# FFN up product by Strassen's scheme, and the residual kept in DRAM, in a one-core hybrid layer

## The chip, the core and the metric

One NeuronCore of a Trainium2 chip runs the whole program. The time is device microseconds of one execution; lower is better. The kernel before was timed three times on the chip, and one more execution was taken by the hardware profiler.

## The reference

One layer on a latent stream of 1024 tokens by 1024 features, with 256 context tokens ahead of it. A token mixer comes first (state-space heads, Fourier mixing, pooling, one output projection), then a feed-forward part that the change is about:

```
a = h @ w_up                      # 1024x1024 @ 1024x5632
a = depthwise 3x3 convolution of a, on a grid of 16 rows x 64 columns, plus bias
val, gate = split(a)              # 2 x 2816 channels
y = (gelu(gate) * val) @ w_down   # 1024x2816 @ 2816x1024
out = layer_norm(ALPHA * x + g2 * y) * ln2_g + ln2_b
```

All inputs and the output are float32.

## The kernel before, in words

Every large product is done in three matmuls: each float32 operand is split into a high part (rounded by ScalarE to fp32r) and a low part (the rest, by GpSimd or VectorE), and high*high, high*low and low*high are added in PSUM. `split` does this. One matmul has a 128x128 stationary part and 512 moving columns.

The feed-forward part works on 22 pairs of channel tiles (`NPAIR`), each a value tile and the gate tile that belongs to it, 44 tiles of 128 channels in all. For a tile, `up_weights` loads 512 KB of `w_up` and splits it, and L1233 does 8 (k tiles) x 3 x 2 (halves q of the tokens, 512 each) = 48 matmuls into a PSUM tile `pu` of 128x1024. There are three PSUM tiles of that size, and two of 128x512. `h2h` and `h2l` are the two parts of the transposed activations.

`conv2d` reads `pu`: ScalarE writes the centre tap with the bias to `cv` (L1176), and VectorE adds the other eight taps, one instruction each (L1184). After the gate tile, ScalarE does the gelu (L1251), GpSimd multiplies by the value (L1252), and the product is split into `gh` and `gl`. `w_down` rows of the pair are loaded, multiplied by the gate vector `g2b` on GpSimd (L1256) and split.

Two pairs make a group. Its down product is cut into 16 units (8 token tiles t, 2 column halves nb): `down_unit` does 6 matmuls into a 128x512 PSUM tile `pdn` (L1158), and VectorE adds it to the residual `xa[t]`, which stays in SBUF (L1161, L1163 the first time). A unit is taken after every second k of an up tile (from tile 6, k 3, to tile 39), so that up and down matmuls alternate; 9 units are left for after the last up tile. There are 9 groups and 144 units; the last four pairs (18 to 21) are multiplied at the end by `last_mm` (L1282, 192 matmuls, `pl`), four token tiles with the pairs taken in turn, then four more, each followed by its layer norm (`post_early`, `post_late`).

The order of instructions on each engine is laid out when the program is built: a planner takes them in program order, but passes over those whose inputs are not due yet by its own costs; `tc.issue_after` adds an edge on one engine. On the chip, each engine and the DMA queue of SP then run their list in that fixed order.

Of the kernel before, what the change touches and what calls it, by code (L numbers as in the profile page):

```python
# [33 lines left out]
def hybrid_layer(  # L34
# [179 lines left out]
    def split(raw, hi, lo, eng=None):  # L214

        S.activation(hi, raw, AF.Identity)  # L216
        (eng or G).tensor_tensor(lo, raw, hi.bitcast(F32), op=ALU.subtract)  # L217
# [856 lines left out]
    def post1(t):
# [3 lines left out]
        V.scalar_tensor_tensor(xa[t], xa[t], st[1], lnb, op0=ALU.mult, op1=ALU.add)  # L1078
# [44 lines left out]
    def up_weights(n):
        ct = chan[n]
        raw = ring("ht2", f"wur{ct}", [P, KD, P])
        nc.sync.dma_start(raw, w_up[:, ct * P : (ct + 1) * P].rearrange("(k p) n -> p k n", p=P))
# [20 lines left out]

    def down_unit(u):

        group, t, nb = u  # L1150
# [4 lines left out]
        for _, gh, gl, wh, wl in group:
            a, b = gh[:, t * P : (t + 1) * P], gl[:, t * P : (t + 1) * P]
            for u_, v_ in ((a, wh), (a, wl), (b, wh)):
                TE.matmul(pt, u_, v_[:, s], start=i == 0, stop=i == n - 1)  # L1158
                i += 1
        if (t, nb) in seen:  # L1160
            V.tensor_tensor(xa[t][:, s], xa[t][:, s], pt, op=ALU.add)  # L1161
# [253 lines left out]
```

## Time and profile before

| | |
|---|---|
| median of 3 runs | 1222.45 us (1218.78 to 1223.37) |
| profiled execution | 1218.48 us, of which the span from first to last instruction is 1216.7 us |
| mean granted TensorE clock | 0.987 |
| TensorE busy | 1154.5 us, 95% |
| VectorE, ScalarE, GpSimd busy | 942.2, 384.3, 455.8 us |
| first up matmul of the feed-forward part (L1194) | at 461.51 us |
| last up matmuls (L1233) | at 1147.21 us |

PE is TensorE, PEld its weight loads, DVE VectorE, ACT ScalarE, POOL GpSimd, SP the engine that issues the DMAs. A row of a timeline has the start, the time, the engine, the line, the operation, output<-inputs, the count, and in brackets how long the engine had been idle and what released it. A row of a table of stages has the length, and for each engine its busy time and instructions.

### The profile page before, as it was taken

To read this page: it belongs to the slowest core of one execution; us is meant where nothing else is said; L and a number is where in the kernel's file an instruction comes from. 1 tells how busy PE (TensorE), PEld (TensorE's weight loads), DVE (VectorE), ACT (ScalarE), POOL (GpSimd) and SP (SyncE) were. 2 spreads that over 40 slices of the span, in tenths; PEclk is the share of its full clock that TensorE was granted. 3 is DMA by queue.
4 is the path that set the end of the run, shared out by engine and by line. 5 is a ranking of instruction groups with operands and counts; after the bars stand their busy time and mean duration, and the time that the engine had idled before them with its cause. 6 is when DMAs were issued, how large, how long until landed. Compare 5 with 4: busy or idle time off the path is not lost.

```text
span 1216.7 us, 14285 instructions
## 1 busy us (share of the span) xinstructions
PE 1154.5 (95%) x5463; PEld 939.9 (77%) x5463; DVE 942.2 (77%) x1360; ACT 384.3 (32%) x575; POOL 455.8 (37%) x243
## 2 busy tenths in 40 slices
PE   4999999899878998999999999999999999999996
PEld 2798887777756787788888888888888888888884
DVE  5788787698898889898777776767777777777947
ACT  2263576711433133332221222221212222222144
POOL 0010122354262044565353535343443535353146
PEclk9999999899988999999999999999999999999998
DMA  9848575566624111221111212021121102121013
GB/s 320 295 141 313 158 211 154 176 216 193 221 78 165 42 36 52 87 70 52 35 52 35 69 35 60 27 69 35 41 64 35 55 33 70 35 69 35 18 36 138
DMA packets 104779, 122.51 MB, mean 101 GB/s; under 512 B 7021, under 2 KB 83579, under 8 KB 104711
## 3 DMA queue, kind: packets, MB, share of 16 engines
q1 hardware_dynamic: 104711, 121.60, 31.3%
q8 instruction: 43, 0.70, 0.2%
q14 instruction: 25, 0.20, 0.1%
HBM read 106.82 MB, written 14.76 MB: 100 GB/s over the span
## 4 chain that ended last, share of the span: by engine, by line
PE 76%; DVE 14%; DMA 5%; ACT 2%; issue 2%; POOL 1%; SPq 0%; DVEq 0%; POOLq 0%; ACTq 0%
PE pu L1233 37%; PE pdn L1158 16%; PE pout L1008 4%; PE pz L342 4%; PE px L443 3%; PE pl L1282 3%; DMA bc<-cs_scratch 2%; PE pf L443 1%; PE pu L1194 1%; DMA wa<-in_w_ada_dram 1%; DVE xa L1077 1%; DVE y L918 1%; PE pm L296 1%; DMA zb_r<-in_w_in_dram 1%; DVE h2h L203 1%
## 5 line engine op out<-in xcount | busy, mean ns | idle before, releaser
L1184 DVE SCALAR_TENSOR_TENSOR cv<-pu,ffc,cv 128x945 f32<-128x945 f32 (+7 forms) x368 | 432.6, 1177 | 21.1 <-ACT cv L1176 11.4
L1233 PE MATMUL pu<-h2h,wul 128*128 128x512 f32 x656 | 205.4, 394 | 0.0
L1233 PE MATMUL pu<-h2h,wuh 128*128 128x512 f32 x656 | 205.1, 394 | 0.0
L1233 PE MATMUL pu<-h2l,wuh 128*128 128x512 f32 x656 | 204.4, 393 | 0.0
L1161 DVE TENSOR_TENSOR xa<-xa,pdn 128x512 f32<-128x512 f32 x128 | 87.4, 683 | 128.2 <-PE pdn L1158 127.9
L217 POOL TENSOR_TENSOR wul<-wur,wuh 128x1024 fp32r<-128x1024 f32 x44 | 106.8, 2429 | 204.3 <-ACT wuh L216 204.2
L1233 PEld LDWEIGHTS pu<-h2h,wuh 128*128 128x128 f32 x656 | 123.2, 188 | 29.0
L1233 PEld LDWEIGHTS pu<-h2l,wuh 128*128 128x128 f32 x656 | 123.2, 188 | 28.6
L1233 PEld LDWEIGHTS pu<-h2h,wul 128*128 128x128 f32 x656 | 123.2, 188 | 27.9
L216 ACT ACTIVATE wuh<-wur 128x1024 fp32r<-128x1024 f32 x44 | 46.3, 1054 | 240.0 <-PE pu L1233 220.7
L1158 PE MATMUL pdn<-wdh,gl 128*128 128x512 f32 x288 | 113.3, 393 | 0.0
L1158 PE MATMUL pdn<-wdl,gh 128*128 128x512 f32 x288 | 113.2, 393 | 0.0
L1158 PE MATMUL pdn<-wdh,gh 128*128 128x512 f32 x288 | 113.1, 393 | 0.0
L1256 POOL TENSOR_TENSOR wdr<-wdr,g2b 128x1024 f32<-128x1024 f32 x22 | 53.1, 2412 | 68.2 <-DMA wdr<-in_ffn_w_down_dram 68.2
L1252 POOL TENSOR_TENSOR cv<-cv,cv 128x1024 f32<-128x1024 f32 (+1 forms) x23 | 53.1, 2310 | 60.6 <-ACT cv L1251 60.6
L217 POOL TENSOR_TENSOR gl<-cv,gh 128x1024 fp32r<-128x1024 f32 (+1 forms) x23 | 53.4, 2322 | 42.3 <-ACT gh L216 41.1
L1158 PEld LDWEIGHTS pdn<-wdh,gh 128*128 128x128 f32 x288 | 54.1, 188 | 12.9
L1158 PEld LDWEIGHTS pdn<-wdh,gl 128*128 128x128 f32 x288 | 54.1, 188 | 12.4
L1158 PEld LDWEIGHTS pdn<-wdl,gh 128*128 128x128 f32 x288 | 54.1, 188 | 12.3
L1176 ACT ACTIVATE cv<-pu,ffc 128x1024 f32<-128x1024 f32 (+3 forms) x46 | 53.2, 1156 | 29.0 <-PE pu L1233 18.8
L1251 ACT ACTIVATE cv<-cv 128x1024 f32<-128x1024 f32 (+1 forms) x23 | 23.5, 1021 | 119.4 <-DVE cv L1184 119.4
L217 POOL TENSOR_TENSOR wdl<-wdr,wdh 128x1024 fp32r<-128x1024 f32 x22 | 52.8, 2413 | 4.7 <-ACT wdh L216 4.7
(357 smaller groups left out, 2082.2 us busy)
## 6 DMA issues: line engine op xcount, KB each, us to landing
wur<-in_ffn_w_up_dram SPq DMA_DIRECT2D x44, 512.0 KB
wad<-in_w_ada_dram SPq DMA_DIRECT2D x32, 512.0 KB
wdr<-in_ffn_w_down_dram SPq DMA_DIRECT2D x22, 512.0 KB
wa<-in_w_ada_dram SPq DMA_DIRECT2D x32, 256.0 KB
bc<-cs_scratch SPq DMA_DIRECT2D x32, 256.0 KB
xr<-in_x_dram SPq DMA_DIRECT2D x8, 512.0 KB
wx_r<-in_w_in_dram SPq DMA_DIRECT2D x8, 512.0 KB
m_scratch<-EU SPq DMA_DIRECT2D x16, 256.0 KB
```

The costliest lines, as they stand in the source:

```text
L216: S.activation(hi, raw, AF.Identity)
L217: (eng or G).tensor_tensor(lo, raw, hi.bitcast(F32), op=ALU.subtract)
L342: TE.matmul(pt[:, j * 512 : j * 512 + ZW], a, b[:, k % 4, :], start=first and i == 0, stop=last and i == 2)
L443: TE.matmul(pt[:, q * 512 : q * 512 + 512], a[:, k, :], b[q][:, k, :], start=k == 0 and i == 0, stop=k == KD - 1 and i == 2)
L1008: TE.matmul(pt[:, nb * 512 : nb * 512 + 512], u, v[:, nb * 512 : nb * 512 + 512], start=first and i == 0, stop=last and i == 2)
L1158: TE.matmul(pt, u_, v_[:, s], start=i == 0, stop=i == n - 1)
L1161: V.tensor_tensor(xa[t][:, s], xa[t][:, s], pt, op=ALU.add)
L1176: S.activation(acc[:, a * 64 : b * 64], pt[:, a * 64 : b * 64], AF.Identity, bias=ffc[:, 396 + ct : 397 + ct], scale=ffc[:, 176 + ct : 177 ...
L1184: last = V.scalar_tensor_tensor(dst, pv[:, r0 + dy : r1 + dy, c0 + dx : c1 + dx], ffc[:, w * 44 + ct : w * 44 + ct + 1], dst, op0=ALU.mult ...
L1233: TE.matmul(pt[:, q * 512 : q * 512 + 512], a[:, k, :], b[q][:, k, :], start=k == 0 and j == 0, stop=k == KD - 1 and j == 2)
L1252: G.tensor_tensor(acc[:, s], acc[:, s], acc_v[:, s], op=ALU.mult)
L1256: G.tensor_tensor(raw, raw, g2b, op=ALU.mult)
```

## The change

For pairs 0 to 6 (`PS` = 7) the up product stays as it was. From pair 7 on (the eighth) a pair is one product with two channel tiles as rows and the two token halves as columns. Of its 8 k tiles, two (0 and 1) are multiplied as before; the other six make two blocks of three, and this 2x2 by 2x2 block product is done with seven block products instead of eight, in Winograd's form of Strassen's scheme. A block product has 3 x 3 = 9 matmuls, so a pair has 63 + 24 = 87 matmuls instead of 96.

- Sums of activations (`combine`, 8 sums and 3 splits for each of three k, on VectorE with ScalarE, in pairs 3 to 5, and `last_t4` after pair 6) go to nine tiles T.
- Sums of weights (`pair_sums`, four sums and five splits on GpSimd with ScalarE for each pair) go to three buffers `S1`, `S2`, `S3`, written for the next pair after the last use in this one; `pair_gate` splits five k tiles of the gate weights.
- `pair` lays out the products. ScalarE copies a partial sum from one PSUM bank to another three times for each pair (X to Z, Z to Y, Z to W), and the product `p7` to SBUF, from where VectorE adds it to both halves of the gate tile. `p7` uses one of the two small PSUM tiles that the units use.
- Eight units are taken in each pair from pair 3 to 20 (`slot`), which is all 144, so none is left for after the last up tile.
- The residual is in DRAM (`xd`): each unit loads its 256 KB, adds, and stores them; the loads are issued three units ahead, into five buffers. It is loaded to SBUF again before `last_mm`.
- `w_down` is loaded and split in halves; three sets of gate buffers instead of four.
- In the last pair the two vertical taps of the convolutions are products on ScalarE that GpSimd adds, and VectorE does six taps instead of eight.

The core of the diff:

```diff
+        nc.sync.dma_start(xd[t * P : (t + 1) * P, :], xa[t])
...
+    KS, PS, TS = 3, 7, 3
+    KD0 = KD - 2 * KS
+    K2, K1 = KD0, KD - KS
...
+    loaded = {}
+    def down_load(u):
+        group, t, nb = u
+        key = group[0][0], t, nb
+        if key not in loaded:
+            loaded[key] = post.tile([P, 512], F32, tag="xt", name=f"xt{group[0][0]}_{t}_{nb}", bufs=5)
+            nc.sync.dma_start(loaded[key], xd[t * P : (t + 1) * P, nb * 512 : nb * 512 + 512])
+        return loaded[key]
...
         group, t, nb = u
+        xt = down_load(u)
+        for v in units[:3]:
+            down_load(v)
+        xs = xd[t * P : (t + 1) * P, nb * 512 : nb * 512 + 512]
         pt = psb(f"pdn{group[0][0]}_{t}_{nb}")
         n = 3 * len(group)
         i = 0
-        s = slice(nb * 512, nb * 512 + 512)
-        for _, gh, gl, wh, wl in group:
+        for _, gh, gl, wd in group:
             a, b = gh[:, t * P : (t + 1) * P], gl[:, t * P : (t + 1) * P]
-            for u_, v_ in ((a, wh), (a, wl), (b, wh)):
-                TE.matmul(pt, u_, v_[:, s], start=i == 0, stop=i == n - 1)
+            for u_, v_ in ((a, 0), (a, 1), (b, 0)):
+                TE.matmul(pt, u_, wd[nb][:, v_, :], start=i == 0, stop=i == n - 1)
                 i += 1
         if (t, nb) in seen:
-            V.tensor_tensor(xa[t][:, s], xa[t][:, s], pt, op=ALU.add)
+            V.tensor_tensor(xt, xt, pt, op=ALU.add)
         else:
-            V.scalar_tensor_tensor(xa[t][:, s], xa[t][:, s], ALPHA, pt, op0=ALU.mult, op1=ALU.add)
+            V.scalar_tensor_tensor(xt, xt, ALPHA, pt, op0=ALU.mult, op1=ALU.add)
             seen.add((t, nb))
-    lastv = [None]
-    def conv2d(pt, ct, rows, acc=None):
+        nc.sync.dma_start(xs, xt)
...
+        own = taps
+        if off:
+            own = [d for d in taps if d[1]]
+            up, dn = off
+            S.activation(up[:, 64:T], pt[:, 0 : T - 64], AF.Identity, scale=factor(-1, 0))
+            vtap[0] = S.activation(dn[:, 0 : T - 64], pt[:, 64:T], AF.Identity, scale=factor(1, 0))
+        def add(a, b):
+            for r0, r1, t in ((max(a, 1), b, up), (a, min(b, 15), dn)):
+                s = slice(r0 * 64, r1 * 64)
+                G.tensor_tensor(acc[:, s], acc[:, s], t[:, s], op=ALU.add)
...
+    def combine(k):
+        ta, b22 = qt("q5", f"ta{k}", [P, 2, 512]), tb[:, 0, :]
+        def whole(dst, q, kt):
+            eng().tensor_tensor(dst, h2h[q][:, kt, :].bitcast(F32), h2l[q][:, kt, :].bitcast(F32), op=ALU.add)
+        b11, b12, b21 = ta[:, 0, :], ta[:, 1, :], t4raw(k)
+        whole(b11, 0, K1 + k)
+        whole(b12, 1, K1 + k)
+        whole(b22, 1, K2 + k)
+        whole(b21, 0, K2 + k)
+        eng().tensor_tensor(b11, b12, b11, op=ALU.subtract)
+        eng().tensor_tensor(b12, b22, b12, op=ALU.subtract)
+        eng().tensor_tensor(b22, b22, b11, op=ALU.subtract)
+        eng().tensor_tensor(b21, b21, b22, op=ALU.subtract)
+        for j, src in ((0, b11), (1, b22), (2, b12)):
+            split(src, Tt[j][k][:, 0, :], Tt[j][k][:, 1, :], eng())
+    def last_t4():
+        for k in range(KS):
+            split(t4raw(k), h2h[1][:, K1 + k, :], h2l[1][:, K1 + k, :], eng())
...
+    STAG = ("q5", "q7", "q13")
...
+    def pair_sums(i):
+        v, g = raws[i]
+        s1, s2, s3 = [qt(tag, f"S{j}_{i}", [P, 8, P], F32R) for j, tag in enumerate(STAG)]
+        sw[i] = {j: [(t[:, k, :], t[:, 3 + k, :]) for k in range(KS)] for j, t in ((1, s1), (2, s2), (3, s3))}
+        sw[i][4] = [(s1[:, 6, :], s3[:, 6, :]), (s1[:, 7, :], s3[:, 7, :]), (s2[:, 6, :], s2[:, 7, :])]
+        a11, a12, a21, a22 = v[:, K1 : K1 + KS, :], v[:, K2 : K2 + KS, :], g[:, K1 : K1 + KS, :], g[:, K2 : K2 + KS, :]
+        G.tensor_tensor(a21, a21, a22, op=ALU.add)
+        G.tensor_tensor(a11, a21, a11, op=ALU.subtract)
+        split(a11, s2[:, 0:3, :], s2[:, 3:6, :])
+        split(a21, s1[:, 0:3, :], s1[:, 3:6, :])
+        G.tensor_tensor(a12, a12, a11, op=ALU.subtract)
+        split(a12[:, 0:2, :], s1[:, 6:8, :], s3[:, 6:8, :])
+        split(a12[:, 2:3, :], s2[:, 6:7, :], s2[:, 7:8, :])
+        G.tensor_tensor(a11, a22, a11, op=ALU.subtract)
+        split(a11, s3[:, 0:3, :], s3[:, 3:6, :])
+    def pair_gate(i):
+        n = KD - KS
+        wh, wl = qt("X0", f"gwh{i}", [P, n, P], F32R), qt("EM1", f"gwl{i}", [P, n, P], F32R)
+        g = raws[i][1]
+        split(g[:, 0:n, :], wh[:], wl[:])
+        gw[i] = wh, wl
...
+    def first_product(i):
+        pv[i] = psa(f"pu{chan[2 * i]}")
+        X, Z = pv[i][:, 0:512], pv[i][:, 512:1024]
+        mm(X, wk(vw[i], K1), hk(0, K1), True)
+        zc[i] = S.copy(Z, X)
+    def pair(i, mid):
+        more = i + 1 < NPAIR
+        if i not in pv:
+            first_product(i)
+        X, Z = pv[i][:, 0:512], pv[i][:, 512:1024]
+        mm(X, wk(vw[i], K2), hk(0, K2))
+        mm(X, wk(vw[i], 0, KD0), hk(0, 0, KD0))
+        if more:
+            slot()
+        mm(Z, sk(i, 2), tk(2))
+        pq[i] = psa(f"pu{chan[2 * i + 1]}")
+        Y, W_ = pq[i][:, 0:512], pq[i][:, 512:1024]
+        S.copy(Y, Z)
+        if more:
+            slot()
+        p7 = psb(f"p7_{i}")
+        mm(p7, sk(i, 3), tk(3), True)
+        s7 = post.tile([P, 512], F32, tag="s7", name=f"s7_{i}")
+        s7c = S.copy(s7, p7)
+        if more:
+            with tc.issue_after(s7c.ins):
+                pair_value(i + 1)
+            slot()
+        mm(Z, sk(i, 1), tk(1))
+        seed = seedw[0] = S.copy(W_, Z)
+        with tc.issue_after(seed.ins):
+            mid()
+            down_split()
+        slot()
+        def z_end():
+            mm(Z, sk(i, 4), hk(1, K2))
+            mm(Z, wk(vw[i], 0, KD0), hk(1, 0, KD0))
+        if more:
+            mm(Y, wk(gw[i], K2), hk(1, K1))
+            slot()
+            z_end()
+            slot()
         else:
+            z_end()
+        acc_v = conv2d(pv[i], chan[2 * i], [(0, 16)], off=None if more else (ring("ht2", "cu0"), ring("ht2", "cd0")))
+        if more:
+            with tc.issue_after(tap[0].ins):
+                pair_sums(i + 1)
+            if i + 2 < NPAIR:
+                pair_raw(i + 2, 0)
+            first_product(i + 1)
+            slot()
         else:
+            mm(Y, wk(gw[i], K2), hk(1, K1))
+        mm(Y, wk(gw[i], 0, KD0), hk(0, 0, KD0))
+        if more:
+            slot()
+        mm(W_, wk(gw[i], 0, KD0), hk(1, 0, KD0))
+        if more:
+            with tc.issue_after(zc[i + 1].ins):
+                pair_gate(i + 1)
+            if i + 2 < NPAIR:
+                pair_raw(i + 2, 1)
+        pqv = pq[i][:].rearrange("p (a n) -> p a n", a=2)
+        V.tensor_tensor(pqv, pqv, s7.unsqueeze(1).broadcast_to([P, 2, 512]), op=ALU.add)
+        return acc_v
+    gtags = [("X1", "X2"), ("X3", "q6"), ("q10", "q11")]
...
+    def down_raw(i, nb, tag=0):
+        s = slice(nb * 512, nb * 512 + 512)
+        raw = post.tile([P, 512], F32, tag="wdr", name=f"wdr{i}_{nb}", bufs=2)
+        nc.sync.dma_start(raw, w_down[i * P : (i + 1) * P, s])
+        G.tensor_tensor(raw, raw, g2b[:, s], op=ALU.mult)
+        half_done.append((i, nb, tag, raw))
...
+        j = i - 1
+        if j < 0:
+            return
+        gated(j, *accs_.pop(j))
+        if j < LASTG:
+            if j % 2 == 1:
+                grp = [(m, *gates[m], wds[m]) for m in (j - 1, j)]
+                units.extend((grp, t, nb) for nb in range(2) for t in range(NT))
+                for m in (j - 1, j):
+                    down_raw(m, 1)
+            else:
+                for m in (j, j + 1):
+                    down_raw(m, 0)
+        else:
+            for m in {LASTG: (0,), LASTG + 1: (1,)}.get(j, ()):
+                down_raw(LASTG, m)
+                down_raw(LASTG + 1, m)
...
+                if n == 2 * PS - 1:
+                    pair_raw(PS, 0)
+                    pair_raw(PS, 1)
+                    pair_value(PS)
...
+            down_split()
+            between(i)
+            if TS <= i < TS + KS:
+                with tc.issue_after(lastv[0].ins):
+                    combine(i - TS)
+            if i == PS - 1:
+                last_t4()
+                pair_sums(PS)
+                pair_raw(PS + 1, 0)
+                pair_gate(PS)
+                pair_raw(PS + 1, 1)
+        else:
+            acc_v = pair(i, lambda: between(i))
+            if i < NPAIR - 1:
+                acc = conv2d(pq[i], chan[2 * i + 1], [(0, 16)])
+            else:
+                acc = conv2d(pq[i], chan[2 * i + 1], [(0, 8), (8, 16)], off=(qt("q3", "cu1"), qt("wl0", "cd1")), early=True)
...
+    for t, tag in enumerate(STAG + ("q2", "X0", "EM1", "q4", "wh0")):
+        xa[t] = qt(tag, f"xl{t}")
+        nc.sync.dma_start(xa[t], xd[t * P : (t + 1) * P, :])
+    down_split()
+    LT = iter(("q9", "q12", "q14", "q8"))
+    for m in range(LASTG + 2, NPAIR):
+        with tc.issue_after((vtap if m == NPAIR - 1 else seedw)[0].ins):
+            for nb in range(2):
+                down_weights(m, nb, next(LT), V if m == NPAIR - 1 else None)
+    gated(NPAIR - 1, *accs_.pop(NPAIR - 1), tags=("q0", "q1"))
...
-        last_acc(t, t != 2)
+        last_acc(t, t != 1)
```

More of the change, by code (lines that the diff above doesn't have):

```diff
@@ new lines, in hybrid_layer, with t4raw @@
+    Tt = [[qt(next(TTAG), f"T{j}_{k}", [P, 2, 512], F32R) for k in range(KS)] for j in (1, 2, 3)]
+    t4r, tb = qt("q13", "t4r", [P, 2, 512]), qt("q7", "tb", [P, 2, 512])
+    eng = cycle(V)
+    def t4raw(k):
+        return t4r[:, k, :] if k < 2 else tb[:, 1, :]
+    def combine(k):
[13 more added lines that the diff above has]
+            split(src, Tt[j][k][:, 0, :], Tt[j][k][:, 1, :], eng())
@@ new lines, in pair_gate, with mm @@
+    def pair_gate(i):
[4 more added lines that the diff above has]
+        gw[i] = wh, wl
+    def mm(dst, a, b, start=False):
+        n = len(a)
+        for k in range(n):
+            for j, (u, w) in enumerate(((0, 0), (0, 1), (1, 0))):
+                TE.matmul(dst, a[k][u], b[k][w], start=start and k == 0 and j == 0, stop=k == n - 1 and j == 2,
+                          skip_group_check=True)
@@ new lines, in wk, with sk, hk, tk @@
+    def wk(w, k0, n=KS):
+        return [(w[0][:, k, :], w[1][:, k, :]) for k in range(k0, k0 + n)]
+    def sk(i, j):
+        return sw[i][j]
+    def hk(q, k0, n=KS):
+        return [(h2h[q][:, k, :], h2l[q][:, k, :]) for k in range(k0, k0 + n)]
+    def tk(j):
+        return [(t[:, 0, :], t[:, 1, :]) for t in Tt[j - 1]]
+    pv, pq, zc = {}, {}, {}
+    def first_product(i):
[3 more added lines that the diff above has]
+        zc[i] = S.copy(Z, X)
@@ L1258, in hybrid_layer, with between @@
-        split(raw[:], wdh[:], wdl[:])
-        group.append((i, gh, gl, wdh, wdl))
-        if len(group) == 2 and i < NPAIR - 3:
-            queue = [(list(group), t, nb) for t in range(NT) for nb in range(2)]
-            group = []
+        gates[i] = gh, gl
+    LASTG = NPAIR - 4
+    accs_ = {}
+    def between(i):
+        j = i - 1
[15 more added lines that the diff above has]
+                down_raw(LASTG + 1, m)
@@ L1268, in hybrid_layer @@
         down_unit(u)
+    for t, tag in enumerate(STAG + ("q2", "X0", "EM1", "q4", "wh0")):
[8 more added lines that the diff above has]
+    gated(NPAIR - 1, *accs_.pop(NPAIR - 1), tags=("q0", "q1"))
+    group = [(m, *gates[m], wds[m]) for m in range(LASTG, NPAIR)]
     NG = len(group)
@@ L1304, in post_sum @@
         for p_, s in parts_of(t):
[L1305 removed]
+            with tc.issue_after(lastv[0].ins) if t == 0 else ExitStack():
+                V.tensor_tensor(xa[t][:, s], xa[t][:, s], p_, op=ALU.add)
     def post_early(t):
```

141 lines of the change are left out of this document (88 added, 53 removed).

## The prediction

> **What bounds the kernel now.** I read the page's engine table, the clock row and the chain first, then a table of stages, the groups of the feed-forward part, and timelines of its two ends. The profiled execution took 1218.48 us, 1.78 us more than its span and 4 us below the median of the runs (1222.45); the sum is made against it. Under 0.5% (6 us) a run of this kernel can't be told from no change.
>
> ```profile
> span 1216.7 us, 14285 instructions
> PE 1154.5 (95%) x5463; PEld 939.9 (77%) x5463; DVE 942.2 (77%) x1360; ACT 384.3 (32%) x575; POOL 455.8 (37%) x243
> ...
> PE 76%; DVE 14%; DMA 5%; ACT 2%; issue 2%; POOL 1%; SPq 0%; DVEq 0%; POOLq 0%; ACTq 0%
> ```
> ```profile
> 527.00:538.00 11.00, 11.00 (x49) 8.94 (x48) 10.72 (x10) 5.01 (x5) 8.37 (x4) 1.00 0.33 95
> 566.00:583.00 17.00, 17.00 (x75) 13.83 (x75) 14.95 (x16) 3.10 (x3) 4.81 (x2) 1.00 0.10 32
> 583.00:599.00 16.00, 16.00 (x71) 13.03 (x70) 12.02 (x12) 3.22 (x4) 7.21 (x3) 1.00 0.11 33
> 600.00:700.00 100.00, 100.00 (x434) 81.13 (x433) 72.71 (x73) 23.21 (x22) 45.48 (x19) 1.00 0.18 53
> 1147.00:1160.00 13.00, 13.00 (x58) 10.63 (x57) 11.88 (x18) 1.86 (x3) 0.00 (x0) 1.00 0.00 0
> 1160.00:1172.00 12.00, 12.00 (x54) 9.64 (x53) 6.00 (x9) 3.26 (x5) 9.56 (x5) 1.00 0.14 46
> 1190.00:1200.00 10.00, 10.00 (x44) 8.07 (x43) 6.69 (x22) 7.96 (x14) 9.39 (x5) 1.00 0.15 58
> 1200.00:1208.00 8.00, 4.82 (x21) 3.57 (x19) 8.00 (x28) 1.65 (x3) 7.84 (x4) 1.00 0.48 192
> ```
> ```profile
> 603.59 2.77 PE pu L1233 x12
> 610.51 1.39 PE pdn L1158 x6
> ```
>
> The chain is TensorE for 76%. In the stage rows (length, then busy time of PE, PEld, DVE, ACT, POOL) PE is busy all of 600 to 700 us, with 434 matmuls in 100 us, and stays so until about 1205. The chain's pieces give the price: 12 up matmuls 2.77 us, 6 down matmuls 1.39 us, 0.231 us each either way. A pair costs 96 + 48 = 144 matmuls, 33.2 us. VectorE has 73% of the time filled, ScalarE 23%, GpSimd 45%. So in pairs 7 to 21 a matmul taken away is worth 0.231 us as long as nothing else sets the pace.
>
> **The products.** 15 pairs with 87 matmuls for 96: 135 fewer, 135 x 0.231 = **31.2 us off**. The other matmuls keep number, shape and weight loads. A pair with its 8 units is then 135 matmuls, 31.2 us.
>
> **What each pair gains in other work.**
>
> ```profile
> L1184 DVE SCALAR_TENSOR_TENSOR cv<-pu,ffc,cv 128x945 f32<-128x945 f32 x120 | 144.1, 1201 | 6.1 <-ACT cv L1176 2.1
> L1161 DVE TENSOR_TENSOR xa<-xa,pdn 128x512 f32<-128x512 f32 x118 | 80.5, 683 | 124.4 <-PE pdn L1158 124.4
> L1184 DVE SCALAR_TENSOR_TENSOR cv<-pu,ffc,cv 128x1008 f32<-128x1008 f32 x60 | 75.9, 1264 | 1.1
> L1184 DVE SCALAR_TENSOR_TENSOR cv<-pu,ffc,cv 128x960 f32<-128x960 f32 x60 | 72.9, 1215 | 1.1
> L217 POOL TENSOR_TENSOR wul<-wur,wuh 128x1024 fp32r<-128x1024 f32 x30 | 72.3, 2410 | 170.9 <-ACT wuh L216 170.9
> L1176 ACT ACTIVATE cv<-pu,ffc 128x1024 f32<-128x1024 f32 x30 | 35.7, 1191 | 0.0
> ```
> ```profile
> 1178.44 1.22 DVE L1305 TENSOR_TENSOR xa<-xa,pl 128x1024 f32<-128x1024 f32 x1 [12.23 <-PE pl L1282]
> 1187.47 0.57 ACT L1294 COPY pl<-xa 128x512 f32<-128x512 f32 x1
> ```
>
> *VectorE.* 16 taps (8 x 1.201 + 4 x 1.215 + 4 x 1.264 = 19.5 us), 8 unit adds (5.5) and the new add of `p7`, 1.22 by the L1305 row: 26.2 us in a pair of 31.2, 84% where it was 75% (25.0 of 33.2). It stays below PE. Counted from a pair's start, the value tile is complete after 96 matmuls (22.2 us); its taps and the adds among them end near 35.5, 4.3 us into the next pair, where ScalarE wants that PSUM tile for Y after 30 matmuls (6.9 us); PE needs Y's copy only 21 matmuls later. The gate's taps end near 19 us of the next pair, and PE wants the tile after 102 (23.6 us). Some 3 to 4 us of slack at both places: cost 0. If that cover goes, VectorE sets the pace: each us that it loses beyond it costs one us a pair.
>
> *ScalarE.* Four copies of 128x512 (0.57 each by the L1294 row) and some nine smaller splits bring it to about 12 us a pair. Each copy lies between two products: Y must be read before Z is written again 21 matmuls later (4.9 us), Z for the next pair 24 matmuls ahead (5.5 us). An instruction ahead in its queue takes 1.2 us at most. Cost 0, except in the last pair, where no units lie between, and W is needed at once: about 1 us.
>
> *GpSimd.* By 2.41 us for 1024 columns: value split 2.4, four sums of 384 (3.6), sum splits 1536 columns (3.6), gate split 640 (1.5), the down weights and gating as before (9.6): 20.7 us, 66%. The sums may start only when the value tile ends (22.2 us) and S2, S3 are wanted 60 and 75 matmuls later (13.9 and 17.3 us); up to there they cost 2.9 and 7.7 us of GpSimd. Hidden. With three gate buffers, each odd pair's `gh` waits for the last unit of an older group; from there to the new group's sixth matmul lie 26 matmuls, 6.0 us, against ScalarE 1.06 + GpSimd 2.41. Up to 1 us in each of seven groups; I take 1 us in all.
>
> *The residual through DRAM.*
>
> ```profile
> 805.32 0.34 SPq L1255 DMA_DIRECT2D wdr<-in_ffn_w_down_dram  x1
> 809.66 2.42 POOL L1256 TENSOR_TENSOR wdr<-wdr,g2b 128x1024 f32<-128x1024 f32 x1 [4.37 <-DMA wdr<-in_ffn_w_down_dram]
> ```
>
> A 512 KB load is used 4.3 us after its issue, at 53 GB/s. Each unit now moves 512 KB in two transfers, about every 3.9 us: 134 GB/s more, 190 in sum, what the row of 1200 to 1208 us shows (192, engines 48% busy). Issue costs SP 0.34 x 16 = 5.5 us of a pair. The load is issued three units (11.7 us) ahead, into the buffer whose store was issued about two units before: 4.3 + 4.3 us fit. What queues on SP behind a store that waits for its add is the next load, and `wur` and `wdr`, which have 10 us and more to spare. Bounds: 0 if the lead holds, and if it doesn't, a unit's add waits, both small PSUM tiles fill, and PE waits with it: up to 4.3 us for each of 144 units. I take 0, the rate and latency being in the rows.
>
> **Pairs 3 to 6 and the passage to pair 7.** `combine` and `last_t4` are 36 VectorE instructions on SBUF.
>
> ```profile
> 442.19 5.09 POOL L204 TENSOR_TENSOR h2l<-h2t,h2h 128x512 fp32r<-128x512 f32 x3 [1.50 <-DVE h2h L203]
> 443.95 2.19 DVE L1078 SCALAR_TENSOR_TENSOR xa<-xa,pn_q,ln1b 128x1024 f32<-128x1024 f32 x1
> 454.26 1.28 DVE L1078 SCALAR_TENSOR_TENSOR xa<-xa,pn_q,ln1b 128x1024 f32<-128x1024 f32 x1
> 488.95 0.68 DVE L204 TENSOR_TENSOR h2l<-h2t,h2h 128x512 fp32r<-128x512 f32 x1
> ```
>
> At 0.68 us they cost 24.5 us. VectorE is full at 527 to 538 and has 4 us of 16 free from 583, when its backlog ends, and 27% of the time to pair 7 (about 671): near 27 us. But L1078, whose vector inputs all lie in SBUF, took 2.19 us beside GpSimd's work and 1.28 without: 0.91 more. With GpSimd busy 45%, that is 36 x 0.45 x 0.91 = 15 us more, and VectorE comes out some 12 us late, against about 20 us by which a convolution may lag before its PSUM tile is wanted. Then S2 can be written only when `last_t4` has read the same buffer, which comes after pair 6's matmuls; PE has 24 X matmuls and up to 8 units to fill with. Bounds 0 and 12; I take **4 us**, nearer the fill.
>
> The Trainium skill's "SBUF — State Buffer", section "Who interferes with whom", says that a VectorE instruction with two SBUF inputs contends with a GpSimd one that reads SBUF, and that the later one waits for the whole of the other. By that, 36 x 0.45 x 1.2 (half of 2.41) = 19 us instead of 15: an estimate; the sum would be 4 us more at worst. The 0.91 us of the rows agrees in kind.
>
> **The tail.** Today 54 matmuls of left units (12.5 us) and 72 of `pl` cover the last gate tile.
>
> ```profile
> 1147.21 0.63 PE L1233 MATMUL pu<-h2h,wul 128*128 128x512 f32 x2
> ...
> 1160.10 0.39 PE L1282 MATMUL pl<-wdh,gh 128*128 128x512 f32 x1
> ```
> ```profile
> 1161.49 0.61 ACT L1251 ACTIVATE cv<-cv 128x512 f32<-128x512 f32 x1
> 1166.84 0.63 ACT L216 ACTIVATE gh<-cv 128x512 fp32r<-128x512 f32 x1 [4.73 <-POOL cv L1252]
> ```
> ```profile
> 1165.50 1.31 POOL L1252 TENSOR_TENSOR cv<-cv,cv 128x512 f32<-128x512 f32 x1
> 1167.55 1.29 POOL L217 TENSOR_TENSOR gl<-cv,gh 128x512 fp32r<-128x512 f32 x1 [0.74 <-ACT gh L216]
> ```
>
> After it the units are gone. Counted from the last up matmul: PE has `pl` 0 to 2 with three pairs, 54 matmuls, 12.5 us; `pl` 3 needs the gate tile's own PSUM. VectorE first ends the value tile's six taps (21 matmuls, 4.9 us, lie after that tile; ScalarE 1.2, taps 7.3: until 4), adds p7 (5.2); ScalarE writes centre and vertical taps (to 9); GpSimd adds two halves of 1.3, behind its four adds for the value tile (5.2 us); VectorE takes 12 half taps of 0.6 to 0.65 us; then gelu 0.61, multiply 1.31, split 0.63 + 1.29 for the first half. With no queueing that is 18.5, with GpSimd's queue 22: PE stands for 6 to 10 us. I take **8**. From there on 138 matmuls and the norms are as before.
>
> ```profile
> 477.83 0.66 PE L187 MATMUL h<-mat,xn 128*128 128x128 f32 x4 [3.32 <-ACT h2t L198]
> ...
> 480.05 0.63 PE L1194 MATMUL pu<-h2h,wuh 128*128 128x512 f32 x1
> 480.47 0.63 PE L1194 MATMUL pu<-h2l,wuh 128*128 128x512 f32 x1
> ```
>
> After a gap of 3.32 us matmuls start 0.42 us apart instead of 0.23, some seven in a row: **1.4 us** after the tail's gap. The eight stores of `xd` and the split load of `mat` ahead of the feed-forward part: 8 x 0.34 us on SP, hidden by its idle time there, of which this row has 46.8 us in one piece: 0.
>
> ```profile
> SPq L1126 <- POOL h2l L204: 48.1, 2, 46.8
> ```
>
> **Sum.** 1218.5 - 31.2 + 1 (last pair) + 1 (gates) + 4 + 8 + 1.4 = 1202.7; taken **1202**. Own range, with the bounds of passage and tail: 1193 to 1211.
>
> **Rivals.**
> *Whole gain*: the planner covers tail and passage. 1218.5 - 31.2 = 1187. For it: PE is at 100% everywhere in the stage today. Against: the 54 covering matmuls are gone.
> *Small waits eat it*: the order is fixed, and PE now waits within a pair for ScalarE, VectorE and GpSimd, each with some 3 to 5 us of slack. 1.2 us lost a pair beyond my sum, 15 x 1.2 = 18: 1220, no change. Against it: the busiest is at 84%.
> *Slower: the residual's loads.* VectorE's add waits for `xt`, PE for the small PSUM tile. From 0.15 us a unit (144 x 0.15 = 21.6) the gain is gone beyond 1224; at 0.25 us it gives 1202 + 36 = 1238. For it: SP runs in order, and a store that waits holds back the loads. Against: 11.7 us of lead.
> *Fewer matmuls, no faster matmul*: shorter groups with other weights each. Excluded by the rows: every matmul loads its weights today (5463 and 5463).
>
> **Chances.** Forecast 0.57, whole gain 0.13, small waits 0.15, slower 0.15. Faster 0.71 (the first two, 0.01 of the third), same 0.13 (of the third), slower 0.16 (the fourth, 0.01 of the third). To hold 8 in 10 the range runs from 1186 to 1221, into the small waits; the residual's rival is left out.
>
> **What would show it.** Right: PE at 9 in every slice up to the tail, about 1977 up matmuls, VectorE above 80% in pairs 7 to 20, a PE gap of 6 to 10 us some 12 us after the last up matmul, with low clock behind it. Wrong: unit adds idle for a DMA (residual); PE idle in each pair, released by ScalarE copies (small waits); no gap (whole gain); a PE gap of 10 us or more near 671.

## The result, and the profile after

The changed kernel takes 1212.6 us (1207.9 to 1216.4) against 1220.0 us (1214.5 to 1223.4) for the kernel before on the same chip: ratio 0.9947, 95% interval 0.9927 to 0.9967. That is 7.4 us less where the sum forecast 15.8. Its profiled execution took 1215.51 us, 12.8 more than the sum's 1202.7.

The head of the page after, and the shares of the chain that ended last:

```profile
span 1213.7 us, 15187 instructions
...
PE 1130.9 (93%) x5328; PEld 918.5 (76%) x5328; DVE 991.2 (82%) x1407; ACT 459.9 (38%) x790; POOL 590.2 (49%) x470
...
PE 58%; DVE 17%; DMA 11%; POOL 4%; ACT 4%; issue 4%; SPq 1%; DVEq 0%; POOLq 0%; ACTq 0%
```

The 135 matmuls are gone (5463 before, 5328 now), and TensorE is still the largest share of the chain. Stage by stage (columns as in the prediction's tables; the last three are the granted TensorE clock, the busy share of the DMA engines and GB/s):

```profile
505.00:590.00 85.00, 85.00 (x369) 69.03 (x368) 78.62 (x74) 26.86 (x34) 46.92 (x32) 1.00 0.38 115
590.00:690.00 100.00, 93.99 (x396) 74.74 (x395) 99.25 (x97) 28.86 (x41) 48.25 (x31) 0.98 0.47 148
690.00:740.00 50.00, 45.78 (x189) 36.16 (x188) 33.23 (x34) 16.45 (x28) 33.03 (x29) 0.97 0.57 178
740.00:1140.00 400.00, 400.00 (x1734) 325.23 (x1733) 321.09 (x321) 147.87 (x245) 286.97 (x246) 1.00 0.57 183
1140.00:1202.00 62.00, 55.92 (x231) 44.01 (x229) 45.67 (x89) 33.83 (x53) 41.73 (x27) 0.94 0.30 108
```

TensorE is full while the new pairs run (740 to 1140). It loses time in three places: 590 to 690, where VectorE is 99% busy; the first 50 us of the new pairs; the tail. What it waited for from 505 to 1202 us (total, times, longest):

```profile
PE pdn L1187 <- DVE xt L1190: 6.1, 4, 4.7
PE pl L1576 <- ACT gh L218: 4.9, 1, 4.9
PE pu L1349 <- ACT pu L1370: 3.4, 1, 3.4
PE pl L1576 <- DVE cv L1234: 0.8, 1, 0.8
```

Three single stands (4.7, 3.4 and 4.9 us) make up most of it, each with slow matmuls behind it. The first, in the timeline:

```profile
664.50 0.62 PE L1521 MATMUL pu<-h2h,wul 128*128 128x512 f32 x2
669.77 1.22 PE L1187 MATMUL pdn<-wd,gh 128*128 128x512 f32 x2 [4.66 <-DVE xt L1190]
```
```profile
660.07 2.91 DVE L1288 TENSOR_TENSOR ta<-h2h,h2l 128x512 f32<-128x512 f32 x2
662.91 3.47 DVE L1288 TENSOR_TENSOR tb<-h2h,h2l 128x512 f32<-128x512 f32 x2
666.30 2.82 DVE L1295 TENSOR_TENSOR ta<-ta 128x512 f32<-128x512 f32 x1
669.04 0.67 DVE L1190 TENSOR_TENSOR xt<-xt,pdn 128x512 f32<-128x512 f32 x1
```
```profile
665.79 2.79 POOL L219 TENSOR_TENSOR wul<-wur,wuh 128x1024 fp32r<-128x1024 f32 x1
```

A down unit wants a small PSUM tile that VectorE has not yet added to the residual. The addition (669.04) stands behind five sums of activations, which take 9.0 us in place of 3.4. VectorE's instructions from 590 to 690 us by form:

```profile
L1295 DVE TENSOR_TENSOR ta<-ta 128x512 f32<-128x512 f32 x3 | 7.5, 2500 | 0.0
L219 DVE TENSOR_TENSOR T<-ta,T 128x512 fp32r<-128x512 f32 x6 | 7.1, 1184 | 0.0
L1288 DVE TENSOR_TENSOR tb<-h2h,h2l 128x512 f32<-128x512 f32 x4 | 7.0, 1778 | 0.0
...
L1297 DVE TENSOR_TENSOR tb<-tb,ta 128x512 f32<-128x512 f32 x3 | 2.0, 678 | 0.0
```

The same operation on the same shape takes 0.678 us in some places and 2.5 us on average in others. All twelve forms of the sums in that view add up to 41 us for 34 instructions; at 0.68 they would be 23.

The pace of the new pairs is in one row, a copy made once in each (15 of them):

```profile
L1391 ACT COPY s<-p x15: 586/588/590, 698.6 to 1138.6; 128x512 f32<-128x512 f32 x15
```

440.0 us for 14 steps, 31.43 us a pair, which still contains the stand at 723 us and its slow matmuls.

### The profile page after: what moved, and what is told of

Same layout as the page of the kernel before. It is cut to its first block, busy times and chain, and to the rows that moved or that the text cites. A ratio compares the mean times of both kernels' runs of the same rounds, so it can differ in the third digit from the quotient of the medians.

```text
span 1213.7 us, 15187 instructions
## 1 busy us (share of the span) xinstructions
PE 1130.9 (93%) x5328; PEld 918.5 (76%) x5328; DVE 991.2 (82%) x1407; ACT 459.9 (38%) x790; POOL 590.2 (49%) x470
## 4 chain that ended last, share of the span: by engine, by line
PE 58%; DVE 17%; DMA 11%; POOL 4%; ACT 4%; issue 4%; SPq 1%; DVEq 0%; POOLq 0%; ACTq 0%
PE pu L1349 20%; PE pdn L1187 13%; PE pu L1521 6%; PE pout L1010 4%; DMA bc<-cs_scratch 3%; PE pl L1576 3%; PE pz L344 2%; PE p L1349 2%; PE px L445 2%; DVE cv L1234 2%; PE pu L1245 1%; DMA wa<-in_w_ada_dram 1%; DMA ctxr<-in_ctx_dram 1%; DMA wdr<-in_ffn_w_down_dram 1%; ACT EU L645 1%
## 5 line engine op out<-in xcount | busy, mean ns | idle before, releaser
L1234 DVE SCALAR_TENSOR_TENSOR cv<-pu,ffc,cv 128x945 f32<-128x945 f32 (+6 forms) x362 | 425.6, 1180 | 74.6 <-ACT cv L1212 64.9
L1187 PE MATMUL pdn<-wd,gh 128*128 128x512 f32 x576 | 182.2, 397 | 6.6 <-DVE xt L1190 6.1
L1187 PEld LDWEIGHTS pdn<-wd,gh 128*128 128x128 f32 x576 | 108.4, 189 | 33.4 <-DVE xt L1190 7.8
L1190 DVE TENSOR_TENSOR xt<-xt,pdn 128x512 f32<-128x512 f32 x128 | 87.3, 682 | 33.3 <-PE pdn L1187 28.2
L1187 PE MATMUL pdn<-wd,gl 128*128 128x512 f32 x288 | 114.1, 396 | 0.0
L219 POOL TENSOR_TENSOR S<-wur,S 128x384 fp32r<-128x384 f32 (+2 forms) x75 | 62.1, 854 | 31.3 <-ACT S L218 30.6
L1349 PE MATMUL pu<-T,S 128*128 128x512 f32 x270 | 67.1, 392 | 0.0
L1349 PE MATMUL pu<-h2h,wuh 128*128 128x512 f32 x150 | 59.9, 400 | 3.4 <-ACT pu L1370 3.4
L1349 PEld LDWEIGHTS pu<-T,S 128*128 128x128 f32 x270 | 50.7, 188 | 11.6
L1349 PE MATMUL pu<-h2h,wul 128*128 128x512 f32 x150 | 59.5, 396 | 0.0
L1349 PE MATMUL pu<-h2l,wuh 128*128 128x512 f32 x150 | 59.2, 395 | 0.0
L1521 PE MATMUL pu<-h2h,wuh 128*128 128x512 f32 x176 | 55.6, 397 | 0.0
```

The source lines that it names most:

```text
L219: return (eng or G).tensor_tensor(lo, raw, hi.bitcast(F32), op=ALU.subtract)
L1187: TE.matmul(pt, u_, wd[nb][:, v_, :], start=i == 0, stop=i == n - 1)
L1190: V.tensor_tensor(xt, xt, pt, op=ALU.add)
L1234: last = V.scalar_tensor_tensor(dst, pv[:, r0 + dy : r1 + dy, c0 + dx : c1 + dx], factor(dy, dx), dst, op0=ALU.mult, op1=ALU.add)
L1349: TE.matmul(dst, a[k][u], b[k][w], start=start and k == 0 and j == 0, stop=k == n - 1 and j == 2, skip_group_check=True)
L1521: TE.matmul(pt[:, q * 512 : q * 512 + 512], a[:, k, :], b[q][:, k, :], start=k == 0 and j == 0, stop=k == KD - 1 and j == 2)
```

## The experiments

Theory S: the gain per pair is whole, and what is missing was lost at a few places. Rival R: the residual's transfers hold units or weights back. Rival P: a pair gives less than 9 matmuls' worth. The row above speaks against P; the runs were to settle S and R. Each run's ratio is to the kernel before, timed beside it on the same chip (medians 1220.1 to 1220.8 us), with its 95% interval.

**No sums.** The sums of `combine` left out of the changed kernel (T is filled by copies on ScalarE):

```
-        whole(b11, 0, K1 + k)
...
-            split(src, Tt[j][k][:, 0, :], Tt[j][k][:, 1, :], eng())
+        for j in range(3):
+            S.activation(Tt[j][k][:, 0, :], h2h[0][:, K2 + k, :].bitcast(F32), AF.Identity)
+            S.activation(Tt[j][k][:, 1, :], h2l[0][:, K2 + k, :].bitcast(F32), AF.Identity)
```

> The kernel after, with the VectorE work of combine left out: the T tiles and the raw T4 are filled by seven ScalarE copies for each k instead of eight sums and three subtractions (so T holds no sums). Theory S (the missing gain is lost at places: VectorE sums beside GpSimd in pairs 3 to 6 about 9 us, start of pair 8 about 5, tail about 7, the rest ahead of the feed-forward part): 8 to 9 us faster than the kernel after (about 1204), and TensorE has no gap between 505 and 685 us. Rival R (the residual's traffic makes the units wait): within 2 us of the kernel after, with the gaps of pairs 3 to 6 still there.

1203.8 us, ratio 0.9864 [0.9834, 0.9895], some 9 us less than with them. From 590 to 690 us TensorE is full and VectorE back at three quarters:

```profile
590.00:690.00 100.00, 100.00 (x433) 80.95 (x432) 74.52 (x75) 26.66 (x38) 45.48 (x34) 1.00 0.52 163
```

**Sums on GpSimd.** All of `combine` there (`eng = cycle(G)`, the remainders of T too).

> The kernel after, with all sums and subtractions of combine on GpSimd instead of VectorE (last_t4 stays on VectorE). Theory S: GpSimd rises by 11 x 1.3 = 14 us to about 30 of the 33 us of a pair, VectorE loses nothing to the shared side any more; 5 to 9 us faster than the kernel after, TensorE without gaps from 590 to 670. Rival R: same as the kernel after within 2 us. If GpSimd can't keep up, the gaps move to pair 7 and the gain is under 3 us.

1229.5 us, ratio 1.0075 [1.0047, 1.0103]: slower than before. From 590 on TensorE is full, but the planner put the sums earlier on GpSimd, and now GpSimd's splits and the convolutions are late there; four stands between 515 and 559 us, 18.7 us in sum, the first and the last of them:

```profile
515.30 1.19 PE L1521 MATMUL pu<-h2h,wuh 128*128 128x512 f32 x2 [4.38 <-DVE cv L1234]
...
558.47 1.22 PE L1521 MATMUL pu<-h2h,wul 128*128 128x512 f32 x2 [7.30 <-POOL wul L219]
```

The run moved 33 of the 36 instructions to another engine, and earlier too (the first to 458 us, where VectorE has it at 588), so it does not tell the two apart. The next runs keep the engine and change the time alone.

**Sums given out three to a tile**, behind the convolutions of tiles 3 to 13, in place of lumps of 11 behind the odd tiles:

```
-            if TS <= i < TS + KS:
-                with tc.issue_after(lastv[0].ins):
-                    combine(i - TS)
+                if n >= 3:
+                    with tc.issue_after(lastv[0].ins):
+                        spread()
```

> The changed kernel, its 36 VectorE instructions of combine (12 sums of high and low part, 12 differences, 12 remainders) given out three behind each convolution of tiles 3 to 13 and three at the end, where they stood in lumps of 11 behind the odd tiles of pairs 3 to 5. Nothing is left out. Theory S (the lumps beside GpSimd fill VectorE and hold the convolutions up, 8.9 us by the kernel without them): a tile leaves VectorE about 4 us free (16.7 less 8 taps of 1.2 and four units' additions of 0.68), three sums at 0.7 to 1.8 us take 2 to 5, so most of the 8.9 us comes back: 1203 to 1208 us, ratio to before 0.986 to 0.990. Rival C (the waits of VectorE for GpSimd's instructions add up to the same sum wherever the sums stand, and VectorE has no 50 us to spare): within 2 us of 1212.6, ratio 0.993 to 0.996.

1215.5 us, ratio 0.996 [0.9943, 0.9977]: nothing gained, as the rival said (at the edge of its ratio), but not for its reason. The stand for `xt` is gone, one for a weight sum `S` has come, and that for ScalarE's copy (the second of the three) is longer:

```profile
PE pu L1361 <- ACT S L218: 6.3, 1, 6.3
PE pu L1361 <- ACT pu L1382: 5.8, 2, 4.8
```
```profile
690.32 0.68 DVE L219 TENSOR_TENSOR T<-ta,T 128x512 fp32r<-128x512 f32 x1
690.92 0.69 DVE L219 TENSOR_TENSOR T<-tb,T 128x512 fp32r<-128x512 f32 x1
691.52 0.68 DVE L219 TENSOR_TENSOR T<-ta,T 128x512 fp32r<-128x512 f32 x1
691.72 1.44 ACT L218 ACTIVATE S<-wur 128x384 fp32r<-128x384 f32 x4 [11.33 <-DVE T L219]
```

The last three remainders stand behind tile 13's convolution, and the first weight sums are written into the buffers `ta` and `tb` that these three read. TensorE waited 6.3 us for it. `tb` is the buffer of which the prediction said that S2 can be written only after `last_t4`.

**The same, finished by tile 12** (four behind tiles 3, 4 and 5, then three):

```
+        for _ in range(4 if n < 6 else 3):
```

> The changed kernel with the VectorE work of combine given out behind tiles 3 to 12 (four behind tiles 3, 4 and 5, then three), so that nothing but the three remainders of T4 is left behind tile 13. Nothing is left out. In the run that gave three to each tile of 3 to 13, TensorE stood 6.3 us at the first pair of the new form, for a sum on ScalarE whose buffer was free only when VectorE had taken the last three remainders, at 692 us, behind tile 13's convolution. Theory S (that is all that ate the gain): the stand and the slow clock behind it go, 7 to 9 us less than that run, 1206 to 1209, ratio to before 0.988 to 0.991. Rival C (what VectorE is spared appears as another wait at the passage, because there GpSimd's sums and remainders are the limit): 1212 to 1216, ratio 0.993 to 0.996.

1207.9 us, ratio 0.990 [0.9885, 0.9914], as S had it. The stand for `S` is gone, the one for `xt` is down to 1.4 us, and TensorE is busy 99.2 of the 100 us from 590 to 690. Ending the same instructions one tile earlier was worth 7.6 us. What is left at the passage is ScalarE's copy:

```profile
PE pu L1361 <- ACT pu L1382: 5.5, 2, 4.7
```

**The passage into the second new pair.** In the changed kernel, first GpSimd's difference, then ScalarE's queue:

```profile
721.48 0.99 POOL L1332 TENSOR_TENSOR wur<-wur,wur 128x384 f32<-128x384 f32 x1
```
```profile
722.51 0.52 ACT L218 ACTIVATE S<-wur 128x384 fp32r<-128x384 f32 x1 [8.84 <-POOL wur L1332]
722.94 0.58 ACT L1370 COPY pu<-pu 128x512 f32<-128x512 f32 x1
```
```profile
723.58 0.51 PE L1349 MATMUL pu<-h2h,wuh 128*128 128x512 f32 x1 [3.44 <-ACT pu L1370]
```

The copy X to Z, which TensorE needs before it may go on in X, stands on ScalarE behind a split that waits for GpSimd. Two runs on it. In the first the lines of the first product were only moved ahead of the sums:

```
+            first_product(i + 1)
             with tc.issue_after(tap[0].ins):
                 pair_sums(i + 1)
...
-            first_product(i + 1)
```

> The changed kernel, the first product of the next pair and its copy Z on ScalarE put ahead of the splits of the next pair's sums of weights in the program. Nothing is left out. Theory S (TensorE's stand of 3.4 us at the passage into the eighth pair, and the slow clock behind it, come from ScalarE's copy queued behind the high part of a sum that waits for GpSimd): the stand goes, 4 to 5 us, 1207 to 1209, ratio 0.989 to 0.991; the other 14 pairs stay at 31.4 us. Rival G (GpSimd itself is late there, by a load of down weights it multiplies; the sums then end later still): the stand moves to the product that needs the sum, 1211 to 1216. A third possibility: the later sums make a wait in every pair, 0.3 to 1 us each, 1212 to 1227.

1211.7 us, ratio 0.9933 [0.9908, 0.9958], the changed kernel's time. ScalarE's order was the same as before, since the planner chooses by its own costs; the stand is there with 3.7 us, so the run settles nothing, though the time lies in G's range. The second keeps the moved lines and adds an edge for the last split:

```
+        with tc.issue_after(zc[i].ins) if i in zc else ExitStack():
             split(a11, s3[:, 0:3, :], s3[:, 3:6, :])
```

> The changed kernel, ScalarE's last split of the next pair's sums held back by an order edge until the copy Z of the next pair's first product is through; in the run that only moved the lines, ScalarE's order stayed as it was and so did the stand of 3.7 us. Nothing is left out. Theory S (TensorE's stand of 3.4 us at the passage into the eighth pair's successor comes from that order alone): the stand and some 2 us of slow clock go, 1206 to 1209, ratio 0.989 to 0.992, other pairs at 31.4 us. Rival G (GpSimd is what is late): the stand moves to the third sum, which is needed some 10 us later and has that much room, so a wait of over 1 us there would speak for it; 1211 to 1214.

1208.6 us, ratio 0.9897 [0.9879, 0.9915]: 4 us. TensorE is full from 690 to 740 us, and no wait appears later in the pair, so GpSimd's lateness itself costs nothing:

```profile
690.00:740.00 50.00, 50.00 (x218) 40.61 (x217) 34.67 (x36) 16.93 (x28) 35.57 (x32) 1.00 0.57 179
```

**Units kept for the tail.** Pair 20 takes none, so that eight are left for later.

> The changed kernel, pair 20 taking none of the down product's units, so that eight (11.3 us of TensorE) are left for the stretch between the last up product and the last down products. Nothing is left out. Theory S (7.4 us are lost there because TensorE has nothing to do until the last gate is through gelu, split and convolution: stands of 0.8 and 4.9 us and slow matmuls behind them): 5 to 7 us less, 1206 to 1208, ratio 0.988 to 0.990. Rival (the units kept pair 20's engines apart: without them the last two pairs' convolutions and splits are late, and the stand comes earlier): 1211 to 1214.

1224.2 us, ratio 1.003 [1.0012, 1.0048], 11.6 us worse than the changed kernel. Of their 48 matmuls 38 ran behind the last up product and 10 within pair 21, which still takes a unit. Waits now stand behind them:

```profile
PE pl L1580 <- DVE cv L1234: 5.3, 1, 5.3
PE pl L1580 <- POOL wd L219: 2.7, 3, 1.3
PE pl L1580 <- ACT wd L218: 2.6, 2, 2.1
```

Both theories missed. The run moved the last gate's own chain too: in its trace GpSimd is still multiplying the last down weights at 1179 us. Whether the tail's stand can be filled without that stays open.

**The constants.** The kernel before with the load of `mat` split as in the change (`ident` alone, then the other three).

> The kernel before, with nothing but the load of the constants split in two transfers (identity first, the other three behind it). Theory F (the split delays what is behind it in the DMA queue): the first up matmul of the feed-forward part starts 2 to 5 us later than 461.5, time 2 to 5 us longer. Rival N (the 4.7 us of the profiled run are scatter from run to run): within 1.5 us of the kernel before.

1221.3 us, ratio 1.0007 [0.9991, 1.0022]: no effect. It bears on the first up matmul, at 466.2 us in the profile after and 461.5 before. In this run's profile it starts at 465.2, as theory F had it, but the time did not follow. And it scatters without the split too: the two runs with sixteen tensors on the kernel before (below) have the same work up to there and start at 466.2 and 458.9 us. Over all profiles the mean is 464.3 us in eleven versions of the changed kernel and 462.9 in six of the kernel before. So most of these 4.7 us, which are in the profiled execution's excess, are scatter and not the change.

**The residual alone.** The kernel before with the residual in DRAM, as in the change:

```
+            loaded[key] = post.tile([P, 512], F32, tag="xt", name=f"xt{group[0][0]}_{t}_{nb}", bufs=5)
+            nc.sync.dma_start(loaded[key], xd[t * P : (t + 1) * P, nb * 512 : nb * 512 + 512])
...
+        for v in units[:3]:
+            down_load(v)
...
+            V.tensor_tensor(xt, xt, pt, op=ALU.add)
...
+        nc.sync.dma_start(xs, xt)
```

> The kernel before, with nothing but the residual in DRAM: stored after the first norm, each unit loads 256 KB three units ahead into five buffers and stores them, loaded again at the end. Theory S: within 2 us of the kernel before, TensorE still without gaps from 505 to 1200, DMA about 190 GB/s. Rival R: slower by 5 us or more, unit adds waiting for the loads.

1250.8 us, ratio 1.025 [1.0223, 1.0278]: 30 us slower, as rival R had it. TensorE waits 18.7 us for additions, but not for rival R's reason: between 700 and 1150 us VectorE has no row that waits for a load of the residual. It is ScalarE that waits there, for weights that come late (the kernel before has no such row). The centre taps on ScalarE, VectorE's taps and its additions follow behind:

```profile
ACT wuh L216 <- DMA wur<-in_ffn_w_up_dram: 92.7, 9, 11.2
```

The DMA queue of SP, in the same stretch and in the timeline:

```profile
SPq L1157 <- DMA x_scratch<-xt: 312.3, 96, 5.6
```
```profile
801.41 0.38 SPq L1181 DMA_DIRECT2D x_scratch<-xt  x1
804.80 0.32 SPq L1157 DMA_DIRECT2D xt<-x_scratch  x1
805.18 0.42 SPq L1181 DMA_DIRECT2D x_scratch<-xt  x1
805.69 0.39 SPq L1128 DMA_DIRECT2D wur<-in_ffn_w_up_dram  x1
808.34 0.32 SPq L1157 DMA_DIRECT2D xt<-x_scratch  x1
```

A load is issued 3.4 us behind the store just ahead of it: SP waits until that store has landed. Three runs asked why. Seven buffers (`bufs=7`):

> The kernel before with the residual in DRAM alone, as in the run that took 1250.8 us, with seven buffers for five, and still three units ahead. Nothing is left out. Theory Q (SyncE's queue is the cause: with five buffers a load for unit u+3 waits until the store of unit u-2 has landed, 3.4 us and 0.32, 23 units in 100 us, so SyncE stands 85 of 100 us and the weights queue behind; with seven it is the store of unit u-4, which has landed): 1218 to 1226, ratio 0.998 to 1.005. Rival T (the traffic itself, 165 against 50 GB/s, makes the weights' loads late): 1240 to 1251, ratio 1.016 to 1.025.

1244.8 us, ratio 1.0202 [1.0174, 1.0229], in the range of rival T. SP still waits (302.6 us): the theory fell. Sixteen tensors in DRAM in place of one, five buffers:

> The kernel before with the residual in DRAM alone, five buffers and three units ahead as in the run of 1250.8 us, the scratch in DRAM declared as 16 tensors of 128x512 in place of one of 1024x1024 (so two stores for one at the start and two loads for one at the end of each row block). Nothing is left out. With seven buffers SyncE still stood 302 us between 700 and 1150 at the loads, each issued 3.4 us behind the store just ahead of it, of another block. Theory Q2 (the load waits for that store because both touch one tensor; SyncE then stands 3.2 us a unit and the weights' loads queue behind): SyncE's wait for stores goes, 1218 to 1226, ratio 0.998 to 1.005. Rival T (traffic, 165 against 50 GB/s): 1240 to 1250.

1235.6 us, ratio 1.0122 [1.0104, 1.0141], between both ranges: half of the loss gone, and SP waits 288.2 us, so Q2 was at most half of it. The order of SP's queue shows the rest: with five buffers and with seven, the planner puts most loads directly behind the store whose buffer it takes, the earliest place there is. So an edge keeps the load one store back:

```
+        with tc.issue_after(stored[0].ins) if stored[0] else ExitStack():
             for v in units[:3]:
                 down_load(v)
...
+        stored[0] = nc.sync.dma_start(xs, xt)
```

> The kernel before with the residual in DRAM alone, five buffers, three units ahead, sixteen tensors, and an order edge that puts the load for unit u+3 behind the store of unit u-1 on SyncE's queue. Nothing is left out. Without the edge the loads stood directly behind the store of unit u-2, whose buffer they take, so SyncE waited out each store's landing (3.2 us a unit, 288 us between 700 and 1150) with the weights' loads queued behind. Theory Q3 (that place in the queue is the cause; with one store more between them the buffer's store has landed): SyncE's wait falls below 100 us there, 1218 to 1226 us, ratio to before 0.998 to 1.005. Rival T (traffic, 165 against 50 GB/s): 1232 to 1240, ratio 1.010 to 1.016.

1221.6 us, ratio 1.0007 [0.9992, 1.0021]: as before the change. SP's wait for stores to land is down to a ninth:

```profile
SPq L1184 <- DVE xt L1180: 158.1, 64, 20.9
...
SPq L1159 <- DMA x_s<-xt: 36.0, 26, 3.2
```

By the first row SP now stands at stores that wait for their additions (2.8 us without the edge). So not all of its standing costs time. What went with the edge is the lateness: ScalarE has no row for late weights any more, and TensorE waits 1.0 us for additions. The traffic is the same (165 GB/s between 700 and 1150 us, 46 in the kernel before), so it was the one tensor and the place in the queue, and not the bytes. The edge without the sixteen tensors was not run.

Does it cost the changed kernel anything? SP waits 223.5 us there for stores to land, between 700 and 1150 us. Sixteen tensors:

> The changed kernel with the scratch of the residual in DRAM declared as 16 tensors in place of one. Nothing is left out. SyncE stands 309 us at the residual's loads in the changed kernel. Theory S (that standing delays nothing TensorE waits for, since a pair takes 31.4 us, 87 and 48 products at 0.231 us each, all the same): 1210 to 1214, the stands at 670, 724 and 1167 us stay. Rival R (the residual's traffic through SyncE's queue makes the weights late and is behind the stands at the passage and in the tail): 1200 to 1208, ratio 0.983 to 0.990.

1212.3 us, ratio 0.993 [0.9917, 0.9943], with all three stands. But SP's wait fell only to 201.8 us, so this run says little; the last one below says more.

**Both repairs**, the sums by tile 12 and the edge for the split:

> The changed kernel with both: the sums given out behind tiles 3 to 12, and ScalarE's last split behind the copy Z. Nothing is left out. Theory S (two separate places, 4.7 and 4.0 us of medians against the changed kernel): they add, 1202 to 1206, ratio to before 0.985 to 0.988. Rival (both relieve the one backlog at the passage, so the second finds nothing left): 1206 to 1209, ratio 0.988 to 0.991.

1202.5 us, ratio 0.9855 [0.9833, 0.9876]. They add (the ratio falls by 0.0092, where it fell by 0.0047 and 0.0050), and this version beats both kernels. Its longest waits, 505 to 1202 us, and its pace:

```profile
PE pl L1593 <- ACT gh L218: 4.9, 1, 4.9
PE pdn L1187 <- DVE xt L1192: 1.4, 1, 1.4
PE pu L1362 <- ACT pu L1383: 0.8, 1, 0.8
```
```profile
L1404 ACT COPY s<-p x15: 586/587/590, 686.6 to 1121.6; 128x512 f32<-128x512 f32 x15
```

435.0 us for 14 steps: 31.07 us a pair.

**Both repairs and the ordered residual:**

> As the changed kernel with both repairs, and the residual's scratch as sixteen tensors with the order edge for its loads. Nothing is left out. Theory S (SyncE's standing delays nothing that TensorE waits for in the changed kernel): as the kernel with the two repairs, within 2 us, 1202 to 1206. Rival R (the standing makes the weights late there too): 3 to 8 us less than with the two repairs, 1195 to 1202, ratio 0.979 to 0.985.

1202.7 us, ratio 0.9854 [0.9835, 0.9874]. SP's wait for stores to land fell from 204.7 to 62.5 us between 700 and 1150, and the time is the same. So in the changed kernel this waiting delays nothing that TensorE waits for.

## Why the prediction was right or wrong

- **135 matmuls at 0.231, 31.2 us:** right. Without stands a pair takes 31.07 us (135 matmuls at 0.230). The rival of small waits in every pair did not come; TensorE is at 400.00 of 400.00 us.
- **Pairs 3 to 6 and the passage to pair 7, taken at 4 us:** mis-sized; 9.0 us were lost by the two profiles (from the first matmul of tile 3 to the first of pair 7: 509.8 to 685.3 us, with one unit more, 1.4 us, against 505.1 to 670.2), and some 9 us of medians came back without the sums. The size of the contention was right: 41 us for 34 instructions is 17.9 more than at 0.68, where the step had 15 for 36. What failed was the slack set against it. "About 20 us by which a convolution may lag" is that of the three large PSUM tiles, and no row shows TensorE waiting for one of them there. The stand at 669.77 us is for one of the two small ones: a unit's addition queues on VectorE behind five sums of a lump of 11, and units come every 4 us or so. The step's free time was a little off as well: 4 us of 16 and 27% of the 72 us to 671 are 23.5 us and not 27, so by its own figures VectorE comes out 16 us late and not 12, still within its 20. The Trainium skill's rule ("SBUF — State Buffer", "Who interferes with whom": the later of the two waits for the whole of the other) gave 19 us of contention. The trace agrees with it: the difference at 666.30 us ends 0.5 us behind the GpSimd instruction that started ahead of it (665.79, 2.79 us), where alone it takes 0.68.
- **The passage to pair 8, put at nothing:** this step failed too. The ScalarE step counted 1.2 us at most for an instruction ahead in the queue, against 5.5 us of lead for the copy Z, and took cost 0. The split ahead of that copy takes 0.52 us, but it stood 8.84 us for GpSimd's difference and the copy stood behind it: 3.4 us of stand and some 2 of slow matmuls. The edge gave 4.0 us of medians.
- **Tail, 8 us and 1.4 for the clock:** stands of 0.77 and 4.94 us and 2.6 us of slow matmuls, 8.3 us in all (from the end of the last up matmul to that of the last `pl`, 51.7 us for 188 matmuls, which at 0.231 are 43.4). The wait was named rightly, ScalarE's split of the last gate, a little over-sized:

```profile
1167.40 1.65 PE L1576 MATMUL pl<-wd,gh 128*128 128x512 f32 x3 [4.94 <-ACT gh L218]
```

- **Last pair and gates, 1 us each:** neither came. No row has TensorE waiting for `gh` before the tail, and in the last pair the planner put four matmuls of `pl` where W was to be waited for:

```profile
1140.45 0.64 PE L1576 MATMUL pl<-wd,gh 128*128 128x512 f32 x2
```

- **The residual through DRAM, 0:** right for this kernel (1202.5 and 1202.7), but by more luck than the step knew. Latency and rate fitted as it said; TensorE is full from 740 to 1140 us while it goes on. It did not see that most loads would stand right behind a store and hold SP. What the kernel before pays with 30 us, the changed one hides. Its weights are loaded further ahead (a pair's first is issued two pairs before), which is the likely reason; no run took that away.
- **Front, 0:** right by the run with two loads of constants; the profile's 4.7 us are mostly scatter.

In pairs 7 to 21 the profile lost 6.1 us in all. From the first matmul of pair 7 to the end of the last up matmul it took 464.6 us against 477.7, which is 13.1 less, where 83 matmuls fewer (135 fewer, but 48 of units and 4 of `pl` more) are 19.2. The passage to pair 8 has 5.0 of it (440.0 us for 14 steps against 435.0 with both repairs).

The sum, against the profiled execution: 4.7 (front, mostly scatter) + 5.0 (9.0 where 4 stood) + 4.1 (pairs 7 to 21: 6.1 where the gates and the last pair had 2) - 1.1 (tail: 8.3 where 9.4 stood) = 12.7; the difference of 1215.5 and 1202.7 is 12.8. Against the medians the front drops out: the other three make 8.0 of the 8.4 us by which 7.4 fall short of 15.8. That 1202 is also what the twice repaired kernel takes is partly chance: it still has the tail's stand, but lost less than the forecast in pairs 3 to 6.

## What to carry to other kernels

When work is added to a busy engine, take the slack from the shallowest buffer whose release queues behind it, and hand the work out in small pieces that end before the next stage needs their buffers. In a queue that runs in order, look at what stands right ahead of each transfer: a load that takes a buffer just stored waits for that store to land, and everything behind it waits too. The planner here, which places work by its own costs, put copy and loads in the wrong place until an edge said otherwise; moving lines in the source changed nothing.
